# One fixed order for the token-stationary products on TensorE, and a fixed place for the combining of seven-product units

## The chip, the cores and the metric

The kernel runs on one core of a Trainium2 chip. TensorE (PE in the profile) multiplies; VectorE (DVE), ScalarE (ACT) and GpSimd (POOL) do the rest; SyncE (SP) issues the transfers of the weights. The metric is the device time of one execution in microseconds, given as the median of several runs. Every engine works through its own queue of instructions in order; between engines, semaphores say when an operand is there or a buffer is free.

## The reference

One block of a streaming encoder over 256 tokens of width 2048, in float32, with 256 memory tokens:

```python
x = x + 0.5 * (silu(n(x) @ w_gate) * (n(x) @ w_up)) @ w_down      # first FFN, hidden width 5632
P = n(x) @ w_in                                                    # pool group, q, k, v, gate, forget gate
x = x + concat(pool_mixer(P), gated_linear_attention(P)) @ w_out
x = x + cross_attention(n(x), n(mem)) @ w_o                        # 4 heads
x = x + 0.5 * swiglu_2(n(x))                                       # second FFN, hidden width 5632
out = n(x)
```

Here n is an RMS norm with a gain of its own at each place. Nearly all of the time goes to the products with the big weight matrices, and these are computed exactly enough for float32: both operands are split into a high and a low part.

## The kernel before, in words

**Weights.** The matrices come in units of 1 MB (512 x 512 numbers each). `Stream` issues a unit's load on SyncE into one of three raw buffers; `split_unit` makes from it a high part wh (ScalarE, L247) and a low part wl = raw - wh (VectorE, L248), with three buffers of each, so the splitting runs at most two units ahead of the products. `in_turn` (L227 to L247) keeps these parts in one order on their engine: every new one is issued after the one remembered in `latest`. `among_weights` puts other work of ScalarE and VectorE at a fixed place in that same order: after the parts that are already in `latest`, and ahead of those that follow.

**Products.** A product of two float32 matrices is three products of parts: high by high, high by low, low by high. In the token-stationary blocks a 128 x 128 piece of the activations (tokens on one side) is held in TensorE and 128 x 512 of the weights streams past: `products` (L323 to L330) issues the three. They go to PSUM, which the kernel uses as four tiles of two banks, 128 x 2 x 512 floats (`ptile`); all blocks, transposes and sums share these four slots. Where a weight is held instead (block_a, L315, for w_in and the query projections), another code issues the matmuls.

**Seven products in place of eight.** `block_s` (L458 to L544) computes 256 tokens by 1024 columns over a list of units. In some units (`sevens`) the 2 x 2 blocks of tokens, depth and columns are multiplied by a scheme of seven products P1 to P7, issued by `seven` (L439 to L456, matmuls L454). Their operands are sums: of the activations (xe, ye, made by `Sums`) and of the weights (T, made by VectorE L431 and split by ScalarE L434 and VectorE L435; xh and xl are the split of the plain three quarters, L247 and L248). P2, P4, P3 and P0 are the "whole" tiles, two PSUM tiles into which plain units accumulate as well. P1, P6, P7 and P5 are the "parts", in two more PSUM tiles opened by the first seven unit (`open_parts`), so while both are open a block holds all four slots. After the last seven unit, `combine` (L512 to L524) takes the parts out of PSUM: ScalarE copies one bank (L516), VectorE adds the others (L517, L518, L521). Where the block ends in the residual x, `early_parts` (L711) then adds the combined parts to x, and the whole tiles go to x by `residual` (L699). In the gate and up blocks, `join` adds the combined parts to the whole tiles (L531).

**Into the residual.** `into_x` (L753 to L770) handles the down projections, w_out and w_o: two halves b = 0 and 1 of 1024 columns of x, each one block_s. Where a norm follows (`gain`), `fold` (L715 to L733) is called for the two column blocks of a half when it is complete: 16 transposes (L722) put a column block into a px tile, ScalarE (L216) and VectorE (L217) split it from there into the next activations xs, and ScalarE takes squares (L733) for the norm. The folds of b = 0 fall into the units of b = 1. For b = 0 the splits of `fold` float; for b = 1 they are placed by `among_weights`.

**What sets the order.** The program is written as a stream of units and operations with delays counted in units. The framework's scheduler (the kernel is built with a simulated timeline) then chooses the final order of each engine: among instructions whose data dependences allow it, it takes the one that its own timeline has ready first. Only what is tied (`in_turn`, `among_weights`, and at the very end `keep_in_program_order`) keeps its written order. Before the change no matmul of `products` or `seven` was tied, and `combine` was tied only where its block does not end in the residual (L540: `st.op(combine if merge else ...)`).

Of the kernel before, what the change touches and what calls it, by code (L numbers as in the profile page):

```python
# [90 lines left out]
def build(ctx, tc, I, out):  # L91
    nc = tc.nc
    st = Stream()
# [23 lines left out]
    def ptile(name):  # L117
        return psum.tile([P, 2, NB], F32, tag="ps", name=name)
# [6 lines left out]
    def uid(s):  # L125
        cnt[0] += 1
        return f"{s}{cnt[0]}"
# [97 lines left out]
    def in_turn(engine, f):  # L225

        if engine in latest:  # L227
            with tc.issue_after(latest[engine].ins):
                latest[engine] = f()
        else:  # L230
            latest[engine] = f()

    def behind_weights(f):

        with tc.issue_after(latest["vector"].ins), tc.issue_after(latest["scalar"].ins):
            return f()

    def among_weights(f):


        scalar, vector = behind_weights(f)
        latest["vector"] = vector
        if scalar is not None:
            latest["scalar"] = scalar
# [80 lines left out]
    def products(ps, act, k, h, wh, wl, first, last):  # L325

        tok = slice(h * P, (h + 1) * P)
        parts = [(act[:, k, 0, tok], wh), (act[:, k, 0, tok], wl), (act[:, k, 1, tok], wh)]
        for i, (a, w) in enumerate(parts):
            nc.tensor.matmul(ps, a, w, start=first and i == 0, stop=last and i == 2)  # L330

    def block_t(srcs, act, evict, delays=(0, 0), amid=None):

# [106 lines left out]
    def seven(banks, act, sums, g, fresh, ends, weights, order):  # L440
        th, tl, rh, rl = weights
        k0, k1, lo, hi = 2 * g, 2 * g + 1, slice(0, P), slice(P, S)
        a11, a12, a22 = ([act[:, k, p, t] for p in range(2)] for k, t in ((k0, lo), (k1, lo), (k1, hi)))
        s3, n1, n4, s2 = sums.parts(g)
        table = {
            "P1": (a11, rh[:, 0], rl[:, 0]), "P3": (n4, rh[:, 1], rl[:, 1]),
            "P2": (a12, rh[:, 2], rl[:, 2]), "P5": (n1, th[:, 0], tl[:, 0]),
            "P7": (s3, th[:, 1], tl[:, 1]), "P6": (s2, th[:, 2], tl[:, 2]),
            "P4": (a22, th[:, 3], tl[:, 3]),
        }  # L450
        for n in order:
            (a, b), wh, wl = table[n]
            for j, (x, w) in enumerate(((a, wh), (a, wl), (b, wh))):
                nc.tensor.matmul(  # L454
                    banks[n], x, w, start=n in fresh and j == 0, stop=n in ends and j == 2
                )  # L456

    def block_s(srcs, act, sums, order, evict, merge=None, sevens=None, late=0):  # L458

        sevens = [g for g in order if g in (sevens or sums.pairs)]
        held, seen = {"banks": {}}, set()

        def banks(*names):
            t = ptile(uid("pt"))
            for i, n in enumerate(names):
                held["banks"][n] = t[:, i]
            return t

        def open_whole():
            if "ps" not in held:
                c = banks("P2", "P4")
                held["ps"] = (banks("P3", "P0"), c)

        def open_parts():
            held["parts"] = (banks("P1", "P6"), banks("P7", "P5"))

        names = {(1, 0): "P2", (1, 1): "P4", (0, 0): "P3", (0, 1): "P0"}

        def unit_s(g):
            def fn(weights):
                if g == sevens[0]:
                    open_parts()
                open_whole()
                fresh = {f"P{i}" for i in range(1, 8)} - seen
                seen.update(fresh)
                ends = ("P1", "P5", "P6", "P7") if g == sevens[-1] else ()
                if "P1" in fresh:
                    order = ("P1", "P7", "P5", "P6", "P2", "P3", "P4")  # L490
                elif merge:
                    order = ("P1", "P2", "P4", "P3", "P5", "P6", "P7")
                else:
                    order = ("P1", "P2", "P3", "P7", "P5", "P6", "P4")
                seven(held["banks"], act, sums, g, fresh, ends, weights, order)
            return fn

        def unit_p(g):
            def fn(wh, wl):
                open_whole()  # L500
                wh, wl = (w.rearrange("p (k j n) -> p k j n", j=2, n=NB) for w in (wh, wl))
                for j in (1, 0):
                    for h in range(2):
                        n = names[j, h]
                        for kk in range(2):
                            products(held["banks"][n], act, 2 * g + kk, h, wh[:, kk, j],
                                     wl[:, kk, j], n not in seen and kk == 0,
                                     g == order[-1] and kk == 1)
                        seen.add(n)
            return fn  # L510

        def combine():  # L512

            e = held["e"] = scope["pool"].tile([P, 4, NB], F32, tag="sg", name=uid("sg"), bufs=2)
            a, b = held["parts"]
            nc.scalar.copy(e[:, 0], a[:, 0])  # L516
            nc.vector.tensor_tensor(out=e[:, 3], in0=a[:, 1], in1=e[:, 0], op=ALU.add)  # L517
            nc.vector.tensor_tensor(  # L518
                out=e[:, 1:3], in0=b, in1=e[:, 3:4].to_broadcast([P, 2, NB]), op=ALU.add
            )  # L520
            last = nc.vector.tensor_tensor(out=e[:, 3], in0=b[:, 1], in1=e[:, 1], op=ALU.add)  # L521
            if merge is not None:
                merge(e[:, 2:4], e[:, 0:2])
            return None, last  # L524

        def join(j):
            if merge is not None:
                evict(j, held["ps"][j])
                return
            e = held["e"][:, 0:2] if j else held["e"][:, 2:4]  # L530
            among_weights(lambda: (None, nc.vector.tensor_tensor(  # L531
                out=e, in0=held["ps"][j], in1=e, op=ALU.add if j else ALU.subtract
            )))
            evict(j, e)

        for g in order:
            if g in sevens:
                st.unit(srcs[g], unit_s(g), split_seven)
                if g == sevens[-1]:
                    st.op(combine if merge else lambda: among_weights(combine), late)  # L540
            else:
                st.unit(srcs[g], unit_p(g))
        for j in (1, 0):
            st.op(lambda j=j: join(j))  # L544

    def block_b(srcs, act, evict, delay=0):

        n_k = 4 * len(srcs)
        held = {}

        def unit(gi):
            def fn(wh, wl):
                if gi == 0:
                    held["ps"] = ptile(uid("pb"))
                wh, wl = (w.rearrange("p (k n) -> p k n", n=NB) for w in (wh, wl))
                for kk in range(4):
                    k = 4 * gi + kk
                    for h in range(2):
                        products(held["ps"][:, h, :], act, k, h, wh[:, kk], wl[:, kk],
                                 k == 0, k == n_k - 1)  # L560
            return fn

        for gi, src in enumerate(srcs):
            st.unit(src, unit(gi))
        st.op(lambda: evict(held["ps"]), delay)
# [187 lines left out]
    def into_x(w, act, scale, gain=None, k0=0, nk=KT, spread_too=True, src=None, way=OUTPUT):  # L753

        for b in range(2):
            st.op(lambda b=b: fetch_x(b, src), 2)
            cols = wwide(w, b * 2 * NB, k0, nk)
            block_s(cols, act, way.sums, way.orders[b], residual(scale, b, 0),
                    early_parts(scale, b), way.sevens[b])
            if gain is not None:  # L760
                for j in range(2):
                    st.op(lambda c=2 * b + j: fold(c, gain), 1)
        if gain is not None:
            st.op(lambda: finish_norm(4, spread_too), 2)
            if spread_too:
                st.op(spread_norm, 3)
# [725 lines left out]
```

## Time and profile before

| | us |
|---|---|
| runs of the kernel, lowest, median, highest | 2101.17, 2102.96, 2103.69 |
| the profiled execution | 2102.94 |
| its span (first to last instruction) | 2101.2 |
| TensorE busy | 2084.1 |
| VectorE busy | 1737.5 |
| ScalarE busy | 1118.8 |

The page of the profile has the busy time of each engine, the chain of work that ended last, and groups of like instructions; a name such as `PE pt L454 <- DVE sg L531: 1.6, 4, 1.0` in the list of waits reads: TensorE, writing a pt tile at line 454, waited for VectorE's line 531 on an sg tile, 1.6 us in total, four times, 1.0 us the longest. A line of the timeline has the start in us from the span's beginning, the duration, engine, line, operation, and out<-in; `x16` says that 16 instructions are put together. An entry in square brackets is the time that the engine stood idle before the instruction, and what ended it. A matmul's duration overlaps the next one's: the rate is read from the starts. A line of windows gives, for a stretch of time, its length, the busy time of each engine with the number of instructions, the clock that TensorE was granted (1.00 is full) and the load of the transfers. All line numbers are those of the kernel before; in the changed kernel the lines behind L330 are higher by two.

### The profile page before, as it was taken

Reading aid. Unit: us, or ns where it says so; the run is one execution under the profiler, and the core shown is the slowest. Engines: PE = TensorE matmul, PEld = TensorE weight load, DVE = VectorE, ACT = ScalarE, POOL = GpSimd, SP = SyncE. Lnnn points to the kernel's source line nnn. Section 1 sums busy time; section 2 is a strip of 40 time slices with the busy share of each in tenths; the row PEclk is TensorE's granted clock in tenths of the full one; section 3 lists DMA queues with packets and bytes.
Section 4 is the critical chain, followed back from the end, with each engine's and each line's share of the span. In section 5 each row is a group of like instructions: output and inputs, shape, how many; then the busy total and the mean of one; then the engine's idle time right before and its main releaser. Section 6 shows DMA issues by size and latency. Waiting matters only on the chain.

```text
span 2101.2 us, 24556 instructions
## 1 busy us (share of the span) xinstructions
PE 2084.1 (99%) x9898; PEld 1741.7 (83%) x9898; DVE 1737.5 (83%) x1578; ACT 1118.8 (53%) x1100; POOL 13.1 (1%) x41
## 2 busy tenths in 40 slices
PE   9999999999999999999999999999999999999998
PEld 7878888888888788888888888888888888888886
DVE  7999899989998777678766455779998999989974
ACT  7655455645554545455645444456554556545544
POOL 0000000000000000000000000000000000000001
PEclk9999999999999999999999999999999999999999
DMA  7556666566656565467754555656566755676673
GB/s 261 202 199 224 237 220 216 185 223 249 213 197 236 191 198 183 158 192 242 262 185 161 163 174 165 219 184 227 190 227 211 245 202 191 225 240 220 206 257 118
DMA packets 143608, 435.94 MB, mean 207 GB/s; under 512 B 9860, under 2 KB 13544, under 8 KB 143112
## 3 DMA queue, kind: packets, MB, share of 16 engines
q1 hardware_dynamic: 143464, 434.38, 61.5%
q8 instruction: 77, 1.26, 0.2%
q14 instruction: 35, 0.29, 0.0%
q10 hardware_dynamic: 32, 0.01, 0.0%
HBM read 417.58 MB, written 16.78 MB: 207 GB/s over the span
## 4 chain that ended last, share of the span: by engine, by line
PE 92%; DVE 5%; issue 2%; ACT 1%; DMA 0%; SPq 0%; DVEq 0%; ACTq 0%
PE pt L330 43%; PE pt L454 21%; PE pa L315 14%; PE pb L330 6%; PE pe L330 3%; DVE wl L248 1%; DVE T L431 1%; PE ph L807 1%; DVE wl L435 1%; DVE xl L248 1%; PE pl L1226 1%; PE pv L1261 1%; ACT wh L247 1%; PE px L722 0%; DVE sg L531 0%
## 5 line engine op out<-in xcount | busy, mean ns | idle before, releaser
L248 DVE TENSOR_TENSOR wl<-raw,wh 128x2048 fp32r<-128x2048 f32 (+2 forms) x278 | 624.0, 2250 | 215.8 <-ACT wh L247 215.1
L247 ACT CAST wh<-raw 128x2048 fp32r<-128x2048 f32 (+2 forms) x278 | 521.2, 1880 | 318.5 <-PE pt L330 83.1
L330 PE MATMUL pt<-wh,xs 128*128 128x512 f32 x1536 | 494.9, 390 | 0.1
L330 PE MATMUL pt<-wh,ys 128*128 128x512 f32 x1344 | 423.4, 390 | 0.0
L434 ACT CAST wh<-T 128x1024 fp32r<-128x1024 f32 x208 | 218.8, 1053 | 347.4 <-DVE T L431 340.8
L330 PEld LDWEIGHTS pt<-wh,xs 128*128 128x128 f32 x1536 | 287.5, 188 | 59.4 <-ACT xs L216 0.4
L315 PE MATMUL pa<-xs,wh 128*128 128x512 f32 x896 | 317.4, 399 | 2.7 <-ACT wh L247 2.5
L330 PE MATMUL pt<-wl,xs 128*128 128x512 f32 x768 | 299.7, 390 | 0.0
L330 PEld LDWEIGHTS pt<-wh,ys 128*128 128x128 f32 x1344 | 251.9, 188 | 52.3 <-ACT wh L247 0.4
L330 PE MATMUL pt<-wl,ys 128*128 128x512 f32 x672 | 261.6, 389 | 0.0
L315 PE MATMUL pa<-xs,wl 128*128 128x256 f32 x896 | 248.4, 281 | 0.0
L435 DVE TENSOR_TENSOR wl<-T,wh 128x2048 fp32r<-128x2048 f32 x104 | 237.6, 2285 | 1.0 <-ACT wh L434 0.8
L315 PEld LDWEIGHTS pa<-xs,wh 128*128 128x128 f32 x896 | 168.1, 189 | 41.8 <-ACT wh L247 3.2
L248 DVE TENSOR_TENSOR xl<-raw,xh 128x1536 fp32r<-128x1536 f32 x104 | 182.2, 1752 | 13.6 <-ACT xh L247 13.6
L315 PEld LDWEIGHTS pa<-xs,wl 128*128 128x128 f32 x896 | 169.8, 190 | 2.1 <-issue 0.2
L330 PEld LDWEIGHTS pt<-wl,xs 128*128 128x128 f32 x768 | 144.2, 188 | 29.9
L247 ACT CAST xh<-raw 128x1536 fp32r<-128x1536 f32 x104 | 153.9, 1480 | 24.2 <-PE pt L454 13.4
L431 DVE TENSOR_TENSOR T<-T,raw 128x512 f32<-128x512 f32 x208 | 143.7, 691 | 5.8
L330 PEld LDWEIGHTS pt<-wl,ys 128*128 128x128 f32 x672 | 126.2, 188 | 26.2
L431 DVE TENSOR_TENSOR T<-raw 128x1024 f32<-128x1024 f32 x104 | 126.9, 1220 | 0.5
L454 PE MATMUL pt<-wh,xs 128*128 128x512 f32 x320 | 124.6, 389 | 0.0
L454 PE MATMUL pt<-wh,xe 128*128 128x512 f32 x320 | 124.5, 389 | 0.0
(236 smaller groups left out, 2430.6 us busy)
## 6 DMA issues: line engine op xcount, KB each, us to landing
raw<-in_ffn_w_down SPq DMA_DIRECT2D x88, 1024.0 KB, 5.6
raw<-in_ffn_w_up SPq DMA_DIRECT2D x80, 1024.0 KB, 5.0
raw<-in_ffn_w_gate SPq DMA_DIRECT2D x77, 1024.0 KB, 5.1
raw<-in_w_in SPq DMA_DIRECT2D x32, 1024.0 KB, 5.3
raw<-in_xattn_w_kv SPq DMA_DIRECT2D x32, 1024.0 KB, 5.2
raw<-in_w_out SPq DMA_DIRECT2D x16, 1024.0 KB, 5.7
raw<-in_xattn_w_q SPq DMA_DIRECT2D x16, 1024.0 KB, 5.7
raw<-in_xattn_w_o SPq DMA_DIRECT2D x16, 1024.0 KB, 5.6
```

What stands on the lines that cost most here:

```text
L247: in_turn("scalar", lambda: nc.scalar.copy(hi, src))
L248: in_turn("vector", lambda: nc.vector.tensor_tensor(out=lo, in0=src, in1=f32(hi), op=ALU.subtract))
L315: nc.tensor.matmul(o, w, x, start=k == 0 and i == 0, stop=last and i == 1)
L330: nc.tensor.matmul(ps, a, w, start=first and i == 0, stop=last and i == 2)
L431: in_turn("vector", lambda: nc.vector.tensor_tensor(out=o, in0=a, in1=b, op=ALU.add))
L434: in_turn("scalar", lambda: nc.scalar.copy(th[:, c], t[:, c]))
L435: in_turn("vector", lambda: nc.vector.tensor_tensor(out=tl, in0=t, in1=f32(th), op=ALU.subtract))
L454: nc.tensor.matmul(banks[n], x, w, start=n in fresh and j == 0, stop=n in ends and j == 2)
L807: nc.tensor.transpose(v[:, i, h * P : (h + 1) * P], g[:, h, i * P : (i + 1) * P], ident)
L1226: nc.tensor.matmul(ps[:, t, :M], ys[:, 4 * h + d, a, tok], xa["K"][:, d, b, :], start=i == 0, stop=i == 11,)
L1261: nc.tensor.matmul(ps[:, d, :S], xa["V"][:, m, a, col], xa["PT"][:, m, b, :], start=i == 0, stop=i == 5,)
```

## The change

Every matmul that `products` and `seven` issue goes through `in_turn("tensor", ...)`: each is issued on TensorE after the one written before it. Matmuls of other code (block_a, transposes, attention) stay free to lie anywhere between them. And `combine` goes through `among_weights` in every block: the copy L516 becomes the last of ScalarE's tied work and the last addition (L521, or the operations of `early_parts` behind it) stays behind it; the next weights' parts are issued after L516 on ScalarE and after L521 on VectorE.

```diff
@@ products
-            nc.tensor.matmul(ps, a, w, start=first and i == 0, stop=last and i == 2)
+            in_turn("tensor", lambda: nc.tensor.matmul(
+                ps, a, w, start=first and i == 0, stop=last and i == 2
+            ))
@@ seven
-                nc.tensor.matmul(
+                in_turn("tensor", lambda: nc.tensor.matmul(
                     banks[n], x, w, start=n in fresh and j == 0, stop=n in ends and j == 2
-                )
+                ))
@@ combine
-            nc.scalar.copy(e[:, 0], a[:, 0])
+            copied = nc.scalar.copy(e[:, 0], a[:, 0])
...
-            return None, last
+            return copied if merge else None, last
@@ block_s
-                    st.op(combine if merge else lambda: among_weights(combine), late)
+                    st.op(lambda: among_weights(combine), late)
```

## The prediction

> **What bounds the kernel now.** I read the page's busy times and its chain that ended last first, then the waits of TensorE, then timelines of TensorE and VectorE where the order of products changes.
>
> ```profile
> span 2101.2 us, 24556 instructions
> PE 2084.1 (99%) x9898; PEld 1741.7 (83%) x9898; DVE 1737.5 (83%) x1578; ACT 1118.8 (53%) x1100; POOL 13.1 (1%) x41
> PE 92%; DVE 5%; issue 2%; ACT 1%; DMA 0%; SPq 0%; DVEq 0%; ACTq 0%
> ```
>
> ```profile
> PE pa L315 <- ACT wh L247: 2.5, 2, 1.5
> PE pt L454 <- DVE sg L531: 1.6, 4, 1.0
> PE pt L454 <- DVE xl L248: 0.5, 2, 0.3
> ```
>
> TensorE is busy 99% of the span and 92% of the chain is its own. Its listed waits for other engines that an order could touch are 2.5, 1.6 and 0.5 us. So a better order has little to win: some 17 us of the span are not matmul (2101.2 - 2084.1). A worse order can lose any amount, because TensorE takes its instructions one after the other: whatever stands first and waits holds up all behind it. The question is therefore not how many instructions move, but whether one is moved ahead of what it waits for.
>
> **The change part by part.** (1) Tying the products of `products` and `seven` into one order adds no instruction: 9,842 matmuls in the built program of either kernel. It moves them, in 188 blocks, by a few to some sixty places. Before, the scheduler set aside products whose operand it thought late and started others; after, they stand as written.
>
> I compared the two built orders and asked of each moved product what it waits for. Three places stand out, all in `into_x` with a gain: the last down part of the first FFN, w_out, and w_o of the attention. There `fold` of the left column half puts 16 transposes into two px tiles; ScalarE L216 and VectorE L217 read them. The next seven-product unit opens two tiles for its parts (P1, P6, P7, P5), and with four PSUM tiles in all these are the two slots that px holds. The built order on TensorE at w_out, in words of the program:
>
> ```
> before: 5 products of seven unit 175 (P2, P3) - 16 transposes (px) - rest of 175's whole
>         products - 48 products of plain unit 176 - 12 parts products of 175 (P1, P7, P5, P6)
> after:  16 transposes (px) - 12 parts products of 175 - whole products of 175 - unit 176
> ```
>
> The first parts product waits for the last L217 of its slot's px tile. Before, it came late enough:
>
> ```profile
> 967.67 0.39 PE L454 MATMUL pt<-xl,ys 128*128 128x512 f32 x1
> 967.90 0.39 PE L454 MATMUL pt<-xh,ys 128*128 128x512 f32 x1
> 968.59 1.91 PE L722 MATMUL px<-ident,x 128*128 128x128 f32 x16
> 970.26 0.48 PE L454 MATMUL pt<-xh,ye 128*128 128x512 f32 x1
> 981.91 0.39 PE L454 MATMUL pt<-xh,ys 128*128 128x512 f32 x1
> ```
>
> ```profile
> 969.59 2.29 DVE L248 TENSOR_TENSOR wl<-raw,wh 128x2048 fp32r<-128x2048 f32 x1 [1.07 <-ACT wh L247]
> 972.93 0.87 DVE L217 SCALAR_TENSOR_TENSOR xs<-px,gains,xs 128x256 fp32r<-128x256 f32 x2
> 976.73 0.88 DVE L217 SCALAR_TENSOR_TENSOR xs<-px,gains,xs 128x256 fp32r<-128x256 f32 x2 [0.15 <-ACT xs L216]
> ```
>
> A product takes 0.23 us from start to start (967.67 to 967.90). The last row of VectorE holds one L217 of each px tile, 0.48 us the first, so the slot is free at 976.73 + 0.48 = 977.21. Before, its first product ran at 981.91, 4.7 us later. After, 5 products no longer stand ahead of the transposes: these begin at 968.59 - 5 x 0.227 = 967.46, and 16 of them, 0.11 us apart, end at 969.2. TensorE then waits 977.21 - 969.2 = 8.0 us with 48 ready products queued behind. The same at the other two places:
>
> ```profile
> 1355.22 1.91 PE L722 MATMUL px<-ident,x 128*128 128x128 f32 x16
> 1367.88 0.39 PE L454 MATMUL pt<-xh,ys 128*128 128x512 f32 x1
> 688.20 1.91 PE L722 MATMUL px<-ident,x 128*128 128x128 f32 x16
> 699.93 0.39 PE L454 MATMUL pt<-xh,ys 128*128 128x512 f32 x1
> ```
>
> ```profile
> 1355.32 2.29 DVE L248 TENSOR_TENSOR wl<-raw,wh 128x2048 fp32r<-128x2048 f32 x1 [3.05 <-ACT wh L247]
> 1362.46 0.88 DVE L217 SCALAR_TENSOR_TENSOR xs<-px,gains,xs 128x256 fp32r<-128x256 f32 x2 [0.16 <-ACT xs L216]
> 694.77 0.88 DVE L217 SCALAR_TENSOR_TENSOR xs<-px,gains,xs 128x256 fp32r<-128x256 f32 x2 [0.15 <-ACT xs L216]
> ```
>
> w_o: nine products leave the front, 1355.22 - 9 x 0.227 + 1.75 = 1354.9; the slot is free at 1362.94; 8.0 us. First FFN: nine leave and two come behind the transposes, 688.20 - 2.04 + 1.75 + 0.45 = 688.4; free at 695.25; 6.9 us. Sum 22.9 us. If a bank is freed alone (two banks to a tile), the first products go about 2 us earlier and the later ones still wait about 1: some 1.2 us less at each, the lower bound; longer by what VectorE might be late, the upper.
>
> What these stalls give back: VectorE and ScalarE, which were late behind the folds, catch up while TensorE stands.
>
> ```profile
> core 0: us, PE busy (x) PEld busy (x) DVE busy (x) ACT busy (x) POOL busy (x), PEclk, DMA share, GB/s
> 984.86:990.74 5.88, 5.67 (x24) 3.97 (x22) 5.75 (x4) 5.43 (x5) 0.00 (x0) 1.00 0.58 161
> 1370.60:1376.00 5.40, 5.04 (x20) 3.41 (x19) 5.26 (x3) 5.15 (x4) 0.00 (x0) 1.00 0.49 150
> 728.97:735.96 6.99, 4.46 (x15) 3.35 (x14) 6.20 (x5) 5.17 (x3) 0.00 (x0) 0.76 0.27 67
> 732.27:735.68 3.41, 3.29 (x10) 2.80 (x11) 3.41 (x3) 1.87 (x2) 0.00 (x0) 0.50 0.46 105
> ```
>
> Each window's loss is its length less its products at full pace. 5.88 - 22 x 0.227 = 0.9; 5.40 - 19 x 0.227 = 1.1; in the third, 14 products, half of them narrow (a pair 0.35 us), 6.99 - 7 x 0.35 = 4.5, which holds the page's 2.5 us of waiting for ACT L247. That third window follows the first stall by 35 us: TensorE comes to it about 8 us later, while the chain that it waits for (the last residual, L733, the fold's splits, the cast of wh) moves by 3 to 4 us only, since the reordered program has the transposes of the right half 32 products earlier. So I take all three back: 6.5 us. Net 16.4.
>
> The fourth row shows the clock: 0.50 for 3.41 us after TensorE was kept waiting. A stall of 7 to 8 us should bring the same, 3.41 / 2 = 1.7 us each, 5.1 in all; bounds 0 and twice that. [...]
>
> (2) Elsewhere in the order: at the boundaries of gate and up blocks the whole tiles are freed by L531, which joins two tiles one after the other.
>
> ```profile
> 96.92 2.35 DVE L531 TENSOR_TENSOR sg<-pt,sg 128x1024 f32<-128x1024 f32 x2
> 97.72 0.39 PE L454 MATMUL pt<-wh,xe 128*128 128x512 f32 x1
> 98.20 0.50 PE L454 MATMUL pt<-xh,xs 128*128 128x512 f32 x1
> 142.59 0.50 PE L454 MATMUL pt<-xh,xs 128*128 128x512 f32 x1 [1.02 <-DVE sg L531]
> ```
>
> Before, a product of another unit was pulled forward to fill this. After, the first whole product is due at 97.7 and the first tile is free at 98.2; the second tile's first product is due at 98.9 and free at 99.27: about 0.35 us more. Ten boundaries have this shape: 3.5 us; bounds 0 and ten times the 1.02 seen.
>
> (3) The combining gets a place among the weights' parts. Instructions stay the same; L521 (0.68) and the first L711 (1.22) go ahead of the next part of the weights, which comes 1.9 us later. The wl of a seven unit is what could be late by it:
>
> ```profile
> 221.44 0.59 ACT L516 COPY sg<-pt 128x512 f32<-128x512 f32 x1 [4.84 <-PE pt L454]
> 227.47 0.68 DVE L521 TENSOR_TENSOR sg<-pt,sg 128x512 f32<-128x512 f32 x1
> 228.07 1.22 DVE L711 SCALAR_TENSOR_TENSOR x<-sg,x 128x1024 f32<-128x1024 f32 x1
> 235.47 2.29 DVE L435 TENSOR_TENSOR wl<-T,wh 128x2048 fp32r<-128x2048 f32 x1
> 236.43 0.39 PE L454 MATMUL pt<-xh,ys 128*128 128x512 f32 x1
> ```
>
> This wl is ready at 237.76, and the strict order wants it at 236.43: 1.3 us late. But ScalarE waited 4.84 us for the last parts product, and the strict order ends the parts 12 products earlier, 2.7 us, so the whole chain starts earlier. I cost it at nothing; with that cover gone it is 1.3 at four down halves (this one and those at 488, 1619, 1871), 5.2 us. What ScalarE and VectorE issue beside this, and the weight loads on SP, change place little; POOL's order is the same.
>
> Sum: 22.9 - 6.5 + 5.1 + 3.5 = +25.0. The profiled execution took 2102.94 us (span 2101.2 and 1.7 around it), the median of the runs is 2102.96, so both give 2128.
>
> **The rivals.** (a) Faster: VectorE reaches the L217s earlier, and the stalls shrink below what they give back. VectorE's queue before them has idle time, 1.07 us at w_out and 3.05 at w_o in the rows above, both waiting for the cast L247. With no stall left the time is 2102.9 - 6.5 = 2096. It decides where the three stalls sum below 6.5 us, that is where the L217s come 5.5 us earlier each; I find at most 3 us to move them by, and that only if the casts, which wait for TensorE to free a weight buffer, come earlier too. (b) The clock isn't lowered: 2128 - 5.1 = 2123. Against it is the 0.50 above, after shorter gaps. (c) The cover of part 3 fails: 2133; nearly the same if the clock stays half for two such spans after a stall (2128 + 5.1). (d) The order does not bite, since the scheduler keeps other products between: 2103. The built order excludes it at the three places, unless the stalls and the returns balance.
>
> **How the numbers follow.** No change that a measurement of this kernel can tell is 0.2%, 4.2 us, so the forecast is six times that. Chances: the sum as it stands 0.58 (2122 to 2134, with banks freed alone and boundaries from 0 to 10); (b) 0.15; (c) 0.15; (a) 0.07; (d) 0.05. The range reaches below (b), with 1.2 us less for each stall and no boundary waits (2116), and a stall shortened by those 3 us of VectorE's idle, to 2112, and above (c) to 2138; outside lie (a), (d) and a little of (c).
>
> **What would show it.** In the changed kernel: L454 waiting 7 to 8 us for VectorE L217 near 690, 975 and 1370 us, each right behind 16 transposes and followed by 3.4 us at clock 0.50; no wait for ACT L247 near 737; L531 waits ten times or so; ScalarE's L516 earlier behind the last seven unit of the left half. The prediction is wrong if those stalls are under 3 us, or if TensorE shows many new waits for wl L248 or L435, which I have at none.

## The result, and the profile after

The changed kernel takes 2130.73 us (median of four runs, 2129.55 to 2131.37) against 2102.26 us for the kernel before beside it: a ratio of 1.0134, with a 95% interval of 1.0117 to 1.0152. The forecast was 2128 (2112 to 2138). The profiled execution took 2131.37 us.

First the page of the changed kernel (span, busy times, chain), then its list of what TensorE waited for (us in total, times, longest).

```profile
span 2129.6 us, 24536 instructions
PE 2090.8 (98%) x9898; PEld 1746.8 (82%) x9898; DVE 1740.5 (82%) x1578; ACT 1118.7 (53%) x1100; POOL 14.3 (1%) x41
PE 84%; DVE 10%; issue 3%; ACT 1%; DMA 1%; SPq 0%; DVEq 0%
```

```profile
PE pt L456 <- DVE xs L217: 22.8, 3, 8.0
PE pt L456 <- DVE sg L533: 3.9, 9, 1.0
```

The work is the same, 9,898 matmuls, and the span is 28.4 us longer. A new line heads the list: products of seven-product units (L454 before, L456 here) wait three times for the fold's split on VectorE, 22.8 us. The list of before had no such line; its waits for ACT L247 (2.5 us) and for xl (0.5 us) are gone. VectorE's share of the chain rose from 5% to 10%, but only 13.5 us of that lie at the three waits. Most of the rise is three stretches of some 42 us each that end at a wait for the join L533 (near 398, 1553 and 1806 us), and each of these waits costs under 1 us: a share of the chain is not time lost.

The three places in TensorE's timeline (at the first with the transposes ahead):

```profile
688.81 1.91 PE L724 MATMUL px<-ident,x 128*128 128x128 f32 x16
690.78 0.40 PE L330 MATMUL pt<-wh,ys 128*128 128x512 f32 x1
698.03 0.76 PE L456 MATMUL pt<-xh,ys 128*128 128x512 f32 x1 [6.85 <-DVE xs L217]
...
984.53 0.77 PE L456 MATMUL pt<-xh,ys 128*128 128x512 f32 x1 [8.01 <-DVE xs L217]
985.09 0.63 PE L456 MATMUL pt<-xl,ys 128*128 128x512 f32 x1
985.52 0.63 PE L456 MATMUL pt<-xh,ys 128*128 128x512 f32 x1
...
1380.08 0.77 PE L456 MATMUL pt<-xh,ys 128*128 128x512 f32 x1 [7.99 <-DVE xs L217]
```

The waits are 6.85, 8.01 and 7.99 us. Behind each the products start 0.43 us apart (985.09 to 985.52), not 0.23: the clock is halved. Windows of the changed kernel around the waits and the half clock:

```profile
core 0: us, PE busy (x) PEld busy (x) DVE busy (x) ACT busy (x) POOL busy (x), PEclk, DMA share, GB/s
691.18:693.30 2.12, 0.00 (x1) 0.00 (x0) 0.64 (x2) 2.12 (x3) 0.00 (x0) 1.00 0.88 254
693.30:703.54 10.24, 5.51 (x13) 4.37 (x14) 4.68 (x7) 2.29 (x6) 0.00 (x0) 0.50 0.48 165
980.02:990.26 10.24, 5.73 (x14) 4.51 (x15) 4.60 (x11) 2.59 (x6) 0.00 (x0) 0.50 0.44 164
1375.97:1386.21 10.24, 6.13 (x15) 4.81 (x16) 4.21 (x10) 2.60 (x6) 0.00 (x0) 0.50 0.29 99
```

At each place the clock is at 0.50 for 10.24 us, three times the 3.41 us seen before the change. TensorE works in the last 5.5 to 6.1 us of it. The loss is the time from the first product to full pace, less its products at 0.227 us: 698.03 to 703.64 with 13 products, 2.7 us; 984.53 to 990.48 with 14, 2.8; 1380.08 to 1386.44 with 15, 3.0. Together 8.4 us.

Where along the program the time came in is read from work that the change left alone, by the first start of the same group in both kernels (duration minimum, median, maximum in ns, then first and last start):

```profile
L984 PE MATMUL pz<-aT,wa x8: 374/374/478, 776.4 to 778.0; 32*128 32x256 f32 x8
L1248 PE MATMUL pt<-ident,P x16: 270/272/301, 1149.7 to 1299.8; 128*128 128x128 f32 x16
L722 PE MATMUL px<-ident,x x96: 270/273/273, 688.2 to 1400.3; 128*128 128x128 f32 x96
```

```profile
L986 PE MATMUL pz<-aT,wa x8: 374/374/478, 783.6 to 785.2; 32*128 32x256 f32 x8
L1250 PE MATMUL pt<-ident,P x16: 270/272/299, 1166.7 to 1316.8; 128*128 128x128 f32 x16
L724 PE MATMUL px<-ident,x x96: 270/273/273, 688.8 to 1427.3; 128*128 128x128 f32 x96
```

The first rows are the kernel before, the second the changed one. It is 7.2 us behind at the gate of the mixer, 17.0 behind at the attention, 27.0 at the last fold, 28.4 at the end. So 9.8 and 10.0 us come in at w_out and w_o, and the second FFN adds 1.4.

### The profile page after: what moved, and what is told of

Same layout as the page of the kernel before. It is cut to its first block, busy times and chain, and to the rows that moved or that the text cites. A ratio compares the mean times of both kernels' runs of the same rounds, so it can differ in the third digit from the quotient of the medians.

```text
span 2129.6 us, 24536 instructions
## 1 busy us (share of the span) xinstructions
PE 2090.8 (98%) x9898; PEld 1746.8 (82%) x9898; DVE 1740.5 (82%) x1578; ACT 1118.7 (53%) x1100; POOL 14.3 (1%) x41
## 4 chain that ended last, share of the span: by engine, by line
PE 84%; DVE 10%; issue 3%; ACT 1%; DMA 1%; SPq 0%; DVEq 0%
PE pt L330 39%; PE pt L456 18%; PE pa L315 15%; PE pb L330 6%; PE pe L330 3%; DVE T L433 2%; DVE wl L437 2%; DVE xl L248 2%; DVE wl L248 1%; DMA raw<-in_ffn_w_up 1%; DVE sg L533 1%; ACT wh L247 1%; PE ph L809 1%; PE pl L1228 1%; PE pv L1263 1%
## 5 line engine op out<-in xcount | busy, mean ns | idle before, releaser
L248 DVE TENSOR_TENSOR wl<-raw,wh 128x2048 fp32r<-128x2048 f32 (+2 forms) x278 | 624.3, 2249 | 246.2 <-ACT wh L247 245.6
L247 ACT CAST wh<-raw 128x2048 fp32r<-128x2048 f32 (+2 forms) x278 | 521.7, 1881 | 359.9 <-PE pt L330 130.4
L330 PE MATMUL pt<-wh,xs 128*128 128x512 f32 x1536 | 486.7, 390 | 0.0
L248 DVE TENSOR_TENSOR xl<-raw,xh 128x1536 fp32r<-128x1536 f32 x104 | 182.1, 1751 | 16.9 <-ACT xh L247 16.9
L247 ACT CAST xh<-raw 128x1536 fp32r<-128x1536 f32 x104 | 153.7, 1478 | 26.4 <-PE pt L456 14.9
L456 PE MATMUL pt<-wh,xs 128*128 128x512 f32 x320 | 124.6, 390 | 0.1
L330 PE MATMUL pb<-wh,xs 128*128 128x512 f32 x384 | 121.6, 392 | 0.0
```

Source lines behind the costliest of these rows:

```text
L247: in_turn("scalar", lambda: nc.scalar.copy(hi, src))
L248: in_turn("vector", lambda: nc.vector.tensor_tensor(out=lo, in0=src, in1=f32(hi), op=ALU.subtract))
L330: in_turn("tensor", lambda: nc.tensor.matmul(ps, a, w, start=first and i == 0, stop=last and i == 2))
L456: in_turn("tensor", lambda: nc.tensor.matmul(banks[n], x, w, start=n in fresh and j == 0, stop=n in ends and j == 2))
```

## The experiments

The theory: a strict order puts products at the head of TensorE's queue whose PSUM slot the fold still holds, at three places, and the half clock follows. The rivals: the strict order costs through late weights' parts at many places; or the combining's place is what costs. Each run is given with its ratio to the kernel before on the same chip.

**The combining alone.** The products are left to the scheduler; only the last two hunks of the change remain.

> The products are left to the scheduler as before; only the combining has its fixed place. My theory (the time went into three waits of TensorE for L217 and the half clock behind them, both from the fixed order of the products): no wait for L217, within 3 us of before, so 2100 to 2105. Rival (the combining pushes the weights' parts back by 1.9 us wherever it stands): at least a third of the loss, 2112 or more.

Measured: 2105.38 us, ratio 1.0014 (1.0005 to 1.0023). No wait for L217. The 2.9 us come from one place, in ScalarE's and TensorE's timelines of this kernel:

```profile
702.88 0.59 ACT L516 COPY sg<-pt 128x512 f32<-128x512 f32 x1 [8.73 <-PE pt L454]
703.36 5.50 ACT L247 CAST wh<-raw 128x2048 fp32r<-128x2048 f32 x3
```

```profile
705.32 0.73 PE L330 MATMUL pt<-wh,ys 128*128 128x512 f32 x2 [1.39 <-ACT wh L247]
707.12 1.22 PE L315 MATMUL pa<-xs,wh 128*128 128x512 f32 x2 [1.07 <-ACT wh L247]
709.56 0.79 PE L330 MATMUL pt<-wl,ys 128*128 128x512 f32 x1 [1.22 <-DVE wl L248]
```

The copy L516 waits for the parts, which the scheduler had postponed, and three casts of weights stand behind it in ScalarE's queue. A fixed place is only as good as the time at which its input comes.

**The order alone.** The changed kernel with the combining floating as before.

> The changed kernel with the combining floating as before; only the order of the products is fixed. My theory (the order makes the loss; what the combining's place alone costs, 2.9 us, is one wait near 705 us that the stall for L217 swallows): three waits for L217 as in the changed kernel, 22 to 23 us, and 2127 to 2133. Rival (the two parts add up): 2130.7 - 2.9 = 2127.8 and below. If the combining's place was what kept wl of the seven-product units in time, waits for L435 of 1.2 us come up.

Measured: 2129.99 us, ratio 1.0133 (1.0119 to 1.0147). Its waits for L217 are the changed kernel's, and there is no wait for wl:

```profile
PE pt L456 <- DVE xs L217: 22.8, 3, 8.0
PE pt L456 <- DVE sg L533: 4.1, 9, 1.0
```

The order makes the whole loss; the combining's place adds nothing to it that can be told (0.7 us between the medians). The three waits near 705 us of the run above are not in the changed kernel's list, so the two costs do not add up; the times alone would not show it.

**Which order.** One run ties the products of the seven-product units alone, one those of the plain units alone; the combining keeps its place in both. The first of the two, as an edit of the changed kernel:

```diff
-            in_turn("tensor", lambda: nc.tensor.matmul(
-                ps, a, w, start=first and i == 0, stop=last and i == 2
-            ))
+            nc.tensor.matmul(ps, a, w, start=first and i == 0, stop=last and i == 2)
```

> Only the products of the seven-product units are tied; those of the plain units are free as before. The built order has the parts products 0 and 1 places behind the transposes, as in the changed kernel. My theory: the three waits for L217 are there, 7 to 8 us each, and 2125 to 2132. Rival (the wait needs the plain products tied too, because otherwise they are run in it): under 2110.

Measured: 2135.89 us, ratio 1.0161 (1.0147 to 1.0174), 4 us above the range's end. Its waits:

```profile
PE pt L454 <- DVE xs L217: 23.0, 3, 8.0
PE pt L454 <- DVE wl L435: 4.8, 4, 1.2
```

The three waits are there in full, so the plain products need not be tied for them. The second line is new: 1.2 us at each of four down halves, 4.8 us, about the 5 us by which this kernel is slower than the changed one. That is the cover that the prediction named. ScalarE's copy of the parts in the changed kernel, then in this one:

```profile
220.57 0.59 ACT L518 COPY sg<-pt 128x512 f32<-128x512 f32 x1 [2.12 <-PE pt L456]
```

```profile
223.35 0.59 ACT L516 COPY sg<-pt 128x512 f32<-128x512 f32 x1 [4.84 <-PE pt L454]
```

With the plain products tied too, the parts end 2.8 us earlier, and wl comes in time.

> Only the products of the plain units are tied; those of the seven-product units are free; the combining keeps its place. The built order has the parts products 48 to 50 places behind the transposes. My theory: no wait for L217, L531 waits as before (1.6 us in all), a wait for the weights' parts near 705 us as with the combining's place alone: 2105 (2102 to 2110). Rival (tying plain products costs by itself, by late wl): above 2112.

Measured: 2104.98 us, ratio 1.0013 (1.0004 to 1.0022). No wait for L217, and the three waits near 705 us of the combining's place. The order of the seven-product units is what brings the loss: with it alone the loss is there in full, without it 2 us are left. With the same ties and the combining floating:

> Only the plain units' products are tied; those of the seven-product units and the combining float as before. My theory: neither the three waits for L217 nor the wait near 705 us that the combining's place brought (casts behind L516 on ScalarE); so the kernel before within its noise, 2101 to 2105, and the combining's place alone accounts for the 2 to 3 us of the two runs that had it without the order of the seven-product units. Rival (tied plain products cost those 2 us): 2105 to 2107, as with the combining placed.

Measured: 2107.36 us, ratio 1.0019 (1.0010 to 1.0028): not the kernel before. By the time the rival is nearer, and tied plain products do cost something here, but through another wait than in the run before. In its list stands

```profile
PE pt L330 <- DVE sg L523: 3.0, 4, 0.8
```

A plain product opens a PSUM slot that the floating combining (L523) leaves late, 0.76 us at each of four down halves. Where the plain products are tied, the place removes this wait and brings the three near 705 us; the two times (1.0013 and 1.0019) can't be told apart. The prediction had put the place down as a possible cost only.

**The 36 products left free.** In the first seven-product unit of the right half, where a fold stands, P1, P7, P5 and P6 are not tied; all else is.

```diff
-                in_turn("tensor", lambda: nc.tensor.matmul(
+                mm = lambda: nc.tensor.matmul(
                     banks[n], x, w, start=n in fresh and j == 0, stop=n in ends and j == 2
-                ))
+                )
+                mm() if n in loose else in_turn("tensor", mm)
...
```

> The changed kernel, but the 12 products P1, P7, P5, P6 of the first seven-product unit of the right half are left free wherever a fold stands (36 of 9,842 matmuls); the scheduler puts them 48 to 53 products behind the transposes again. My theory: the waits of 22.8 us and the half clock behind them (about 9 us) go, the waits of before behind the folds (0.9, 1.1 and 4.5 us) come back, the boundaries of gate and up keep some 3 us: 2105 (2102 to 2108). Rival (the strict order costs through late weights' parts at many places): above 2115.

Measured: 2111.36 us, ratio 1.0045 (1.0032 to 1.0057). The waits for L217 are gone and 19.4 of the 28.5 us with them, so these 36 products carry most of the loss; but I had expected over 25. Its waits:

```profile
PE pt L456 <- DVE sg L535: 4.2, 9, 1.0
PE pa L315 <- ACT wh L247: 2.1, 2, 1.3
PE pt L456 <- DVE xl L248: 2.0, 2, 1.1
PE pt L330 <- DVE wl L248: 1.7, 1, 1.7
PE pt L456 <- DVE wl L437: 1.5, 2, 0.8
...
PE pt L330 <- ACT wh L247: 1.2, 1, 1.2
```

Weights' parts are late behind all three folds, more than in the kernel before, where the scheduler still had other products to put there. These waits and those for the join (12.7 us) are 8.1 us more than the like ones of the kernel before (4.6), most of the 10.6 us by which the span is longer; and the half clock behind the first fold lasts 6.83 us, not 3.41. So the rival was partly right: the strict order has a price of late parts. In the changed kernel these waits are not listed; that VectorE and ScalarE catch up in the three long waits fits this.

**The unit moved later, the order strict.**

```diff
-    OUTPUT = IntoX((0, 4), (0, 4), ((1, 2, 3, 4, 0, 5, 6, 7), (1, 0, 2, 3, 4, 5, 6, 7)),
+    OUTPUT = IntoX((0, 4), (0, 4), ((1, 2, 3, 4, 0, 5, 6, 7), (1, 2, 3, 0, 4, 5, 6, 7)),
...
-    REST = IntoX((0,), (2,), ((1, 2, 3, 4, 0, 5), (1, 2, 0, 3, 4, 5)), ((0,), (0,)))
+    REST = IntoX((0,), (2,), ((1, 2, 3, 4, 0, 5), (1, 2, 3, 0, 4, 5)), ((0,), (0,)))
```

> The changed kernel with its strict order whole, but in the right half the first seven-product unit is the fourth unit (w_out, w_o: units 1, 2, 3, 0, 4 to 7; last FFN part: 1, 2, 3, 0, 4, 5), so that 46, 46 and 34 products stand between the transposes and the first parts product. My theory: 46 x 0.227 = 10.4 us and 34 x 0.227 = 7.7 us cover the 8.0 and 6.9 us, no wait for L217 over 0.5 us: 2100 to 2108, as with the products left free. Rival (it is the strictness, not the place): above 2115.

Measured: 2116.87 us, ratio 1.0068 (1.0055 to 1.0080): by the time alone the rival's range. The waits tell more. At w_out and w_o the wait for L217 is gone with the order still strict, as the theory has it; one of 4.8 us stays at the last part of the first FFN, where the last pair of splits, which float, now runs behind one more wl on VectorE (L248 at 698.88, the pair at 701.09). And xl and xh come late (2.6 and 1.8 us); the mean clock of the run is 0.996, against 0.998 before. Place decides, but a new place has its own late parts.

**A dose from TensorE's side.** The 9 whole products of the first seven-product unit ahead of its 12 parts products.

```diff
-                if "P1" in fresh:
+                if "P1" in fresh and merge:
+                    order = ("P2", "P3", "P4", "P1", "P7", "P5", "P6")
+                elif "P1" in fresh:
```

> The changed kernel, but the first seven-product unit of a block that ends in x issues its 9 whole products (P2, P3, P4) ahead of its 12 parts products: a dose of the supposed cause. My theory: the parts reach the wait 9 x 0.227 = 2.0 us later, so the three waits for L217 shrink by 2.0 us each, from 6.9, 8.0, 8.0 to about 5, 6, 6; all still long enough for the half clock: 2130.7 - 6 = 2124.7 (2121 to 2128). Rival (the wait ends with something on TensorE itself): the waits keep their length, 2130.

Measured: 2122.86 us, ratio 1.0096 (1.0082 to 1.0110).

```profile
PE pt L456 <- DVE xs L217: 16.1, 3, 6.0
```

```profile
core 0: us, PE busy (x) PEld busy (x) DVE busy (x) ACT busy (x) POOL busy (x), PEclk, DMA share, GB/s
697.74:701.15 3.41, 3.41 (x10) 2.63 (x9) 0.00 (x0) 0.00 (x0) 0.00 (x0) 0.50 0.32 122
977.63:984.46 6.83, 3.71 (x9) 3.00 (x10) 3.76 (x9) 3.28 (x6) 0.00 (x0) 0.50 0.49 196
```

The waits shrink by 6.7 us in all, 2 us or a little more each, so their end does lie outside TensorE. The time fell by 7.9 us between the medians and 9.5 between the profiled executions. The half clock at the three places is now one, two and two times 3.41 us in place of three each; read as above it costs 5.3 us in place of 8.4, and 6.7 + 3.1 is close to the 9.5.

**A dose from VectorE's side.** The fold's splits of the left half placed among the weights' parts, `among_weights(parts)` for every column block; and then both doses together.

> The changed kernel with its strict order whole, but the fold's splits (L216, L217) of the left half get a fixed place among the weights' parts, as those of the right half have: on VectorE the 8 L217 then stand one tile after the other, ahead of a wl part (2.2 us) or three T parts (2.4 us) that ran before or between them. My theory (the wait lasts until VectorE gets to the last L217 of a slot): the first slot is free about 5.5 us earlier, the second about 3; the waits for L217 shrink from 22.8 us to 6 to 10 in all, too short for three windows of half clock; the weights' parts come later by 4 us, so some of the 6.5 us that the stalls gave back is lost: 2111 (2105 to 2118). Rival (it is TensorE's own order that sets the length): 2128 to 2132.

Measured: 2123.74 us, ratio 1.0099 (1.0085 to 1.0113). The length does hang on VectorE's order, but far less than forecast: 16.5 us of waits remain, in six pieces. VectorE and TensorE of this kernel at w_out:

```profile
974.44 0.48 DVE L217 SCALAR_TENSOR_TENSOR xs<-px,gains,xs 128x256 fp32r<-128x256 f32 x1 [0.53 <-ACT xs L216]
975.46 0.48 DVE L217 SCALAR_TENSOR_TENSOR xs<-px,gains,xs 128x256 fp32r<-128x256 f32 x1 [0.54 <-ACT xs L216]
...
980.99 0.48 DVE L217 SCALAR_TENSOR_TENSOR xs<-px,gains,xs 128x256 fp32r<-128x256 f32 x1 [0.54 <-ACT xs L216]
```

```profile
978.14 0.47 PE L456 MATMUL pt<-xh,ys 128*128 128x512 f32 x1 [3.38 <-DVE xs L217]
981.62 0.77 PE L456 MATMUL pt<-wh,ys 128*128 128x512 f32 x1 [2.25 <-DVE xs L217]
```

The slots come free one after the other, and the splits run 1.0 us apart, since each L217 now waits about 0.54 us for its L216 on ScalarE. The expectation had no term for that.

> Both remedies on the strict order: the fold's splits placed, and the whole products ahead of the parts products in the first seven-product unit of blocks that end in x (2.0 us more cover at each place). My theory: hardly any wait for L217 (under 4 us in all), no half clock there; left are the boundaries of gate and up (3.4 us) and late weights' parts behind the folds: 2107 (2103 to 2113). It would be below 2102 only if the late parts cost less than in the kernel before (6.5 us), which I do not expect.

Measured: 2122.73 us, ratio 1.0096 (1.0082 to 1.0110), with 15.0 us of waits: missed. In the built order one, six and nine of the nine whole products now stand ahead of the transposes. Those push the splits back too, so they cover nothing of the wait once the splits follow the transposes closely.

**The wait filled.** The fold's transposes issued three times over.

> The changed kernel with the transposes of the left half's folds issued three times over (same values): 32 more on TensorE at each of the three places, 3.5 us of work inside the wait, which ends when L217 has read px. My theory: VectorE starts its L217 3.7 us behind the transposes, so the ends of the waits do not move by more than 1 us and the idle time shrinks from 6.9, 8.0, 8.0 to about 3.4, 4.5, 4.5 at no cost; the clock falls later or not at all, so that of the 2.9 us that the half clock costs behind each wait a part is saved: 2123 to 2130. Rival (the half clock does not come from the idle time): same products at 0.43 us apart for as long, 2130.7; rival (the wait is for PE's own transposes): it lengthens by 3.5 us each, 2141.

Measured: 2135.04 us, ratio 1.0154 (1.0140 to 1.0168): 4.3 us slower than the changed kernel (the two intervals overlap a little), where I had expected no loss. The idle time shrank to 14.8 us, but the 10.5 us of filling were more than that by 2.5: the transposes of the second px tile come later, and at the last FFN part the first L217 waited for its L216 (1.75 us). The clock fell all the same, to 0.50 for 6.83 us at each place, at waits of at most 4.8 us. Whether a fully covered wait keeps the clock is not settled by it.

## Why the prediction was right

The place, the sign and the mechanism were right. By its terms, measured against its own sum:

- The three stalls: forecast 6.9, 8.0 and 8.0, measured 6.85, 8.01 and 7.99. Reading the first free moment of the slot from VectorE's L217 rows of before, and the arrival from the count of products moved, was enough: from the first transpose to the first product of the parts it is 9.1, 9.8 and 9.8 us by the prediction, 9.2, 9.9 and 9.9 in the changed kernel. At the first place this was in part luck: VectorE's order is another one there, with two of the eight L217 ahead of the last wl L248 and not behind it, and the sum came out the same.
- The returns of 6.5 us: the waits for L247 and xl are gone from the list. By stages the account closes with them: up to 776 us 7.2 us came in, and 6.85 of stall, 2.7 of clock and 2.0 to 2.6 from ahead of it (see the boundaries), less 4.5, make 7.0 to 7.7; at w_out 8.01 + 2.8 - 0.9 = 9.9 for 9.8; at w_o 7.99 + 3.0 - 1.1 = 9.9 for 10.0. But they came with the stalls: without them, in the run with the 36 products free, a strict order has more late parts than before.
- The clock was the term that was mis-sized: 5.1 us forecast, 8.4 measured, 2.7 to 3.0 at each place. The prediction took one span of 3.41 us at 0.50 behind each stall, its author's estimate from the one row at hand; here each stall brought three, of which 5.5 to 6.1 us fell on the work after it. So the second condition of rival (c), half clock for two such spans, nearly came true, and the time lies between the sum's 2128 and this rival's 2133. Twice the forecast was its upper bound. That a stall of this length always brings three is not so: with the order alone the same three stalls cost 6.5 us of clock, and the first only 1.7, as forecast.
- The boundaries: forecast 3.5, measured 2.9 to 3.5. The second FFN, behind the last fold, adds 1.4 us. Ahead of the first fold the changed kernel is 2.0 us behind, read from the transposes of the FFN, which may move between the products, or 2.6, read from the number of matmuls started; 0.5 of it was there at 39 us, before any of the ten boundaries. The listed waits for L531 rose by 2.3 us (1.6 to 3.9), from four to nine, but these stand at only five of the ten boundaries.
- The combining at nothing: right beside the order (0.7 us between the medians with and without), and for the reason given: the parts end 2.8 us earlier, forecast 2.7. Without that cover it is 4.8 us, forecast 5.2, as the run with only the seven-product units tied shows. That it costs 2.9 us by itself, through casts behind L516 on ScalarE, was not foreseen.

22.8 + 8.4 + 2.9 + 0.5 - 6.5 = 28.1 us, or 28.7 with the longer reading of the boundaries, of 28.4. Of the rivals, the faster one fell with the stalls in full; that the clock is not lowered fell with the 0.50; a failed cover did not occur. The half clock lasted one, two and three times 3.41 us in these runs; at the first stall of the changed kernel it began after 2.12 us without a matmul.

What stays open: how much of the 28.4 us could be had back with the order kept. No run of these was faster than the kernel before; the best with any order tied was 2 us slower.

## What to carry to other kernels

Before fixing an order by hand on an engine that works strictly in sequence, as TensorE did here (it stood for 6.85 to 8.01 us with other products queued behind the one that waited), ask of each instruction what frees its destination, not only what brings its operands: a scheduler that had postponed a few products may have done so because another block still held their buffer. Look for it where two phases share PSUM slots. A long wait hides other lateness, so taking it away can give back less than its length: here 19.4 us for 22.8 us of waits.

## What had not been expected of the hardware

At the stalls the half clock came in whole multiples of 3.41 us: 10.24 us at the changed kernel's three of 6.85 to 8.01 us; with the whole products first, 3.41 at the stall of 4.2 and 6.83 at that of 5.9. In the changed kernel it began 2.1, 3.5 and 3.9 us after TensorE fell idle, and it ended 5.5 to 6.1 us after work began again, so that the two stalls of 8 us cost 2.8 and 3.0 us more.

The length of the stall does not settle it alone. In the run with the order alone the first stall is 6.85 us again, up to 697.54, and the half clock lasts two spans, not three:

```profile
core 0: us, PE busy (x) PEld busy (x) DVE busy (x) ACT busy (x) POOL busy (x), PEclk, DMA share, GB/s
694.05:700.88 6.83, 3.34 (x8) 2.70 (x9) 3.43 (x7) 1.73 (x4) 0.00 (x0) 0.50 0.58 199
```

Within each of these two runs the starts of the half clock at the three stalls lie on a grid of 3.413 us, a third of 10.24. In the changed kernel 693.30, 980.02 and 1375.96 are 84 and 116 times that apart; with the order alone 694.05, 977.36 and 1373.30 are 83 and 116 times that apart. That it matters where on this grid a stall falls is an inference from these two runs; the forecasts could not know it. At their stalls of 6.85 to 8.0 us, the clock's cost went from 1.7 to 3.0 us.

The clock also fell at waits of 1.07 to 1.46 us. In the kernel before, the clock fell at 732.27, in the second of two waits of 1.46 and 1.07 us; in the run with the combining alone at 706.71, in the second of two of 1.39 and 1.07, for 6.83 us, and products start 0.43 us apart there as well:

```profile
711.01 0.63 PE L330 MATMUL pt<-wl,ys 128*128 128x512 f32 x1
711.43 1.05 PE L330 MATMUL pt<-wh,ys 128*128 128x512 f32 x2
```

But in the run with the plain products tied and the combining floating, the same two waits (1.45 and 1.07 us) brought none: the clock is 1.00 from 730 to 740 us.
